# One decoder layer on one core: the halo copy ahead of the scaling, and every up-projection block of the first pass unsplit

## The chip, the core and the metric

The kernel is one program on one core of a Trainium2 chip. It has five instruction streams that run beside each other: TensorE (PE in the profile, with its weight loads on a row of their own, PEld), VectorE (DVE), ScalarE (ACT), GpSimd (POOL) and SyncE (SP), which here issues every DMA. Each stream works in its own order; semaphores tie them together. The metric is the device time of one execution in microseconds, and lower is better.

## What is computed

One layer of a hybrid decoder runs over 2048 prompt tokens and 64 sample tokens (8 sequences of 8) that share all weights. Width is 1024, the feed-forward width 2816. Cut to what matters here:

```
h = rmsnorm(x);  u = h @ w_in                          # mixer: convolutions, delta rule
x = x + concat(conformer, deltanet) @ w_out
up, ffn_buf_new = causal_dwconv(rmsnorm(x) @ w_up, ffn_buf, ffn_conv_w, ffn_conv_b)   # 3 taps
gate, val = split(up, 2)
x = x + (silu(gate) * val) @ w_down
x = x + (p @ w_ple) * sigmoid(x @ w_ple_gate)
return rmsnorm(x) and the new states
```

`w_up` is 1024 x 5632. The three-tap convolution over time needs, for each of the 5632 channels, the last two up-projected columns of the tokens before.

## The kernel before

**Passes.** The tokens go through in six passes of 2, 3, 3, 3, 3 and 2 tiles of 128 (`NTS`, L30); the last one also takes the 64 sample tokens. Channels lie on partitions and tokens run along the free axis, so a pass is `n` = 256, 384, 384, 384, 384 and 320 columns wide. While a pass does its feed-forward, the mixer of the pass after it is merged between the steps (L1437).

**Split weights.** A full-precision product is made of three products in the reduced type `F32R`: a weight block of 128 x 1024 comes as float32 (`raw`, 512 KB), ACT rounds it to a high half, POOL subtracts to get the low half (`split`, L230), and `gemm` (L282) multiplies high by high, high by low and low by high: 24 matmuls for a block of eight 128-deep pieces. The two halves, 1 MB together, are written to DRAM (`halves`, L255), and later passes read them back instead of splitting again. All of this is in `wblock` (L242).

**Unsplit blocks.** In the first pass three of four `w_up` blocks go another way (L243): the float32 block is loaded straight into the weight tile `w`, and `up_gemm` (L1218) multiplies it in plain float32 by `q.hf`, the float32 copy of the normed input that only this pass keeps. There are 44 `w_up` blocks, 22 for gates and 22 for values; 33 of them go unsplit. The set `seen` remembers them: at its next use, in the second pass, such a block is loaded as `raw`, split, and its halves are written. The other 11, those with the block number a multiple of four, are split in the first pass and read back as halves in the second.

**Buffers.** The tile `w` has three buffers, and so has `xio`, which `raw` shares with input rows, output rows and the layer-norm tiles. `get` (L262) keeps three blocks loaded ahead. SP issues every load and store in one order and waits in it: a store of halves waits for POOL's part of the split, and what stands behind it waits too.

**A feed-forward step.** `half` (L1224) takes one `w_up` block: the gemm into a PSUM bank `g` (three buffers, columns 2 onward), the copy of the two halo columns from `ffh` into columns 0 and 1 (L1230, ACT), the scaling by tap 2 with the bias into `y` (L1231, ACT), the two other taps as multiply-adds on DVE that read the bank (L1239), and the copy of the bank's last two columns into `ffh` for the next pass (L1242, ACT). `gate` then applies Silu to `y`, `val` multiplies by the gate on DVE and splits the product into `fbuf` (ACT the high half, POOL the low), and `down` (L1258) multiplies by `w_down` and adds into `X`. The down steps of a group of two are queued one group later.

The framework schedules the recorded instructions engine by engine, so the order on an engine is not that of the source.

Of the kernel before, what the change touches and what calls it, by code (L numbers as in the profile page):

```python
# [16 lines left out]
P = 128  # L17
# [25 lines left out]
def step_kernel(  # L43
# [63 lines left out]
    def act(out, in_, f=AF.Copy, **kw):  # L107
        A.activation(out, in_, f, **kw)  # L108
# [99 lines left out]
    ffh = const([P, 2 * FT, 2 + 2 * NSQ], name="ffh")  # L208
# [28 lines left out]
    halves, seen = {}, set()  # L237
# [2 lines left out]
        return wp.tile([P, 2, KD, P], F32R, tag="w", name=nm("w"), bufs=3)  # L240

    def wblock(key, src, hi_e="a", lo_e="g", nk=KD):  # L242
        if key[0] == "w_up" and key[1] // P % 4 and key not in seen:  # L243
            seen.add(key)
            w = wp.tile([P, KD, P], F32, tag="w", name=nm("w"), bufs=3)
            SY.dma_start(w, src)
            return w
        w = w_tile()
        if key in halves:
            SY.dma_start(w.bitcast(F32), halves[key])  # L250
        else:
            raw = raw_tile("raw")
            SY.dma_start(raw if nk == KD else raw.rearrange("p (k o) c -> p k (o c)", k=nk), src)
            split(raw, w[:, 0], w[:, 1], hi_e, lo_e)
            halves[key] = hw.tile([P, 2, KD, P], F32, tag=nm("halves"), name=nm("halves"))  # L255
            SY.dma_start(halves[key], w.bitcast(F32))
        return w[:, 0], w[:, 1]
# [949 lines left out]
    def units_f(q):  # L1207
        n, np_, sam = q.n, q.np, q.sam
        out = []
        z = {}  # L1210

        def begin():
            z["f"] = big.tile([P, 2 * FG * 2 * NMAX], F32R, tag="F", name=nm("fbuf"))
            if sam:
                z["st"] = big.tile([P, 2 * FT, 2 * NSQ], F32, tag="zs", name=nm("fst"))
                load_T("fst", [st_ffn[0].rearrange("s r c -> (s r) c")], 2 * DFF, z["st"])

        def up_gemm(ps, w):  # L1218
            if isinstance(w, tuple):
                return gemm_w(ps, w, halfs(q.hT2), 0, n)  # L1220
            for k in range(KD):
                mm(ps, w[:, k, :], q.hf[:, k, :], k == 0, k == KD - 1, skip=False)

        def half(col):  # L1224
            ffS = W["ff"]
            w = get()
            y = r_tile("y")
            ps = gbank()
            up_gemm(ps[:, 2:2 + n], w)
            act(ps[:, 0:2], ffh[:, col, 0:2])  # L1230
            act(y[:, :n], ps[:, 2:2 + n], AF.Identity, scale=ffS[:, col, 2:3], bias=ffS[:, col, 3:4])  # L1231
            if sam:
                srow = srow_tile()
                G.tensor_copy(srow[:, :, 0:2], z["st"][:, col, :].rearrange("p (s r) -> p s r", r=2))
                act(srow[:, :, 2:2 + LSQ], sv(ps[:, 2 + np_:2 + n]))
                G.tensor_copy(ffh[:, col, 2:18].rearrange("p (s r) -> p s r", r=2), srow[:, :, 8:10])
            for tap in (1, 0):
                c = ffS[:, col, tap:tap + 1]
                stt(V, y[:, 0:np_], ps[:, tap:tap + np_], c, y[:, 0:np_], MUL, ADD)  # L1239
                if sam:  # L1240
                    stt(V, sv(y[:, np_:n]), srow[:, :, tap:tap + LSQ], c, sv(y[:, np_:n]), MUL, ADD)
            act(ffh[:, col, 0:2], ps[:, np_:np_ + 2])  # L1242
            return y

        def ff_ap(slot, hl, j, a, b):
            base = ((slot * FG + j) * 2 + hl) * NMAX
            return z["f"][:, base + a:base + b]

        def gate(f):
            z["g"] = y = half(f)  # L1250
            act(y[:, :n], y[:, :n], AF.Silu)

        def val(f, slot, j):
            y = half(FT + f)
            tt(V, y[:, :n], y[:, :n], z["g"][:, :n], MUL)
            split(y[:, :n], ff_ap(slot, 0, j, 0, n), ff_ap(slot, 1, j, 0, n))

        def down(nk, slot, i):  # L1258
            w = get()
            m = KD // nk  # L1260
            for o in range(m):
                ps = bank() if q.ip == 0 and o % 2 else gbank()
                gemm(ps[:, :n], (lambda k: w[0][:, k * m + o, :], lambda k: w[1][:, k * m + o, :]),
                     (lambda k: ff_ap(slot, 0, k, 0, n), lambda k: ff_ap(slot, 1, k, 0, n)), nk)
                xs = q.X[:, i * m + o, 0:n]
                tt(V, xs, xs, ps[:, :n], ADD)

        out.append(((), begin))
        pend = []
        for g0 in range(0, FT, FG):  # L1270
            slot = (g0 // FG) % 2
            nk = min(FG, FT - g0)
            for j in range(nk):
                f = g0 + j
                out.append(((("w_up", f * P),), lambda f=f: gate(f)))
                out.append(((("w_up", (FT + f) * P),), lambda f=f, slot=slot, j=j: val(f, slot, j)))
            out += pend
            pend = [((("down", g0, i),), lambda nk=nk, slot=slot, i=i: down(nk, slot, i)) for i in range(nk)]
        return out + pend
# [191 lines left out]
```

## Time and profile before

| what | value |
|---|---|
| median of three runs | 3144.91 us (3142.12 to 3147.45) |
| profiled execution | 3150.69 us, span 3149.0 us |
| busy PE / PEld / DVE / ACT / POOL | 94% / 92% / 67% / 34% / 21% of the span |
| mean granted TensorE clock | 0.974 |
| moved by DMA | 745.19 MB, mean 237 GB/s |
| chain that ended last | PE 65%, DVE 7%, DMA 4%, ACT 1% |

Busy time of PE is of modelled matmul ends, so the start of one row to the start of the next is the better measure of what a block takes. In the time line, the number in brackets at a row's end is how long the engine sat idle before it and for what. The profiled execution took 5.8 us longer than the median of the runs.

In the span, the first pass does its feed-forward from about 332 to 627 us, the second from about 723 to 1192 us; the third, fourth and fifth follow at 522 us each, and the last feed-forward ends at about 3090 us.

### The profile page before, as it was taken

Reading aid. Unit: us, or ns where it says so; the run is one execution under the profiler, and the core shown is the slowest. Engines: PE = TensorE matmul, PEld = TensorE weight load, DVE = VectorE, ACT = ScalarE, POOL = GpSimd, SP = SyncE. Lnnn points to the kernel's source line nnn. Section 1 sums busy time; section 2 is a strip of 40 time slices with the busy share of each in tenths; the row PEclk is TensorE's granted clock in tenths of the full one; section 3 lists DMA queues with packets and bytes.
Section 4 is the critical chain, followed back from the end, with each engine's and each line's share of the span. In section 5 each row is a group of like instructions: output and inputs, shape, how many; then the busy total and the mean of one; then the engine's idle time right before and its main releaser. Section 6 shows DMA issues by size and latency. Waiting matters only on the chain.

```text
span 3149.0 us, 49670 instructions
## 1 busy us (share of the span) xinstructions
PE 2968.5 (94%) x18418; PEld 2888.1 (92%) x18418; DVE 2121.8 (67%) x5378; ACT 1074.2 (34%) x2702; POOL 664.2 (21%) x957
## 2 busy tenths in 40 slices
PE   5979899787999999999999999999999999998998
PEld 5979788787998999999999999999999999898998
DVE  6986889755776686668567656857577866743444
ACT  3434333434222443422234332223342222423223
POOL 3422343334222422200101210110131110111111
PEclk8989899988999999999999999999999999998999
DMA  7645888577786767666756577765677775666885
GB/s 227 202 135 198 247 249 271 204 261 268 263 270 233 272 227 250 247 240 237 236 205 230 205 274 244 242 216 197 238 250 249 258 250 189 221 231 227 297 294 211
DMA packets 300407, 745.19 MB, mean 237 GB/s; under 512 B 51241, under 2 KB 213546, under 8 KB 225023
## 3 DMA queue, kind: packets, MB, share of 16 engines
q1 hardware_dynamic: 300167, 742.03, 68.7%
q8 instruction: 146, 2.39, 0.3%
q14 instruction: 94, 0.77, 0.1%
HBM read 607.75 MB, written 134.57 MB: 236 GB/s over the span
## 4 chain that ended last, share of the span: by engine, by line
PE 65%; DVE 7%; DMA 4%; ACT 1%; issue 1%; POOL 0%; SPq 0%; ACTq 0%; DVEq 0%
PE g L89 57%; PE d L89 3%; DMA w<-halves 3%; PE m L89 2%; PE d L93 1%; DVE h L96 1%; PE m L93 1%; DVE y L96 1%; DMA raw<-in_w_up_dram 1%; DVE cacc L96 0%; DVE H L96 0%; DVE X L100 0%; DVE hT L105 0%; DVE tv L105 0%; DVE X L105 0%
## 5 line engine op out<-in xcount | busy, mean ns | idle before, releaser
L89 PE MATMUL g<-hT,w 128*128 128x384 f32 (+2 forms) x9048 | 1575.3, 332 | 35.6 <-ACT hT L108 9.4
L89 PEld LDWEIGHTS g<-hT,w 128*128 128x128 f32 x9048 | 1499.2, 190 | 46.7 <-ACT hT L108 11.1
L89 PE MATMUL g<-fbuf,w 128*128 128x384 f32 (+2 forms) x2904 | 535.1, 334 | 20.7 <-ACT w L108 8.3
L96 DVE SCALAR_TENSOR_TENSOR y<-g,ffS,y 128x384 f32<-128x384 f32 (+1 forms) x528 | 300.7, 570 | 332.3 <-ACT y L108 244.5
L89 PEld LDWEIGHTS g<-fbuf,w 128*128 128x128 f32 x2904 | 478.6, 189 | 30.2 <-ACT ffh L108 8.9
L96 DVE SCALAR_TENSOR_TENSOR cacc<-H,cfS,cacc 128x384 f32<-128x384 f32 (+1 forms) x696 | 453.0, 651 | 10.3 <-ACT cacc L108 3.1
L105 DVE TENSOR_TENSOR X<-X,g 128x384 f32<-128x384 f32 (+2 forms) x532 | 276.3, 524 | 244.7 <-PE g L89 241.9
L105 POOL TENSOR_TENSOR fbuf<-y,fbuf 128x384 fp32r<-128x384 f32 (+2 forms) x132 | 136.1, 1031 | 716.4 <-ACT fbuf L108 676.4
L105 POOL TENSOR_TENSOR w<-raw,w 128x1024 fp32r<-128x1024 f32 x90 | 218.6, 2430 | 297.7 <-ACT w L108 284.6
L89 PE MATMUL g<-mx,w 128*128 128x384 f32 (+2 forms) x1152 | 198.6, 332 | 15.9 <-DMA w<-halves 15.6
L89 PEld LDWEIGHTS g<-mx,w 128*128 128x128 f32 x1152 | 191.8, 195 | 17.8 <-issue 11.5
L89 PE MATMUL g<-x,w 128*128 128x384 f32 (+2 forms) x1152 | 202.5, 329 | 5.9 <-ACT w L108 4.6
L108 ACT ACTIVATE g<-ffh 128x2 f32<-128x2 f32 x264 | 45.7, 173 | 444.0 <-PE g L89 441.8
L89 PEld LDWEIGHTS g<-x,w 128*128 128x128 f32 x1152 | 190.4, 194 | 6.7 <-ACT w L108 5.0
L108 ACT ACTIVATE y<-g,ffS 128x384 f32<-128x384 f32 (+2 forms) x264 | 169.7, 643 | 13.5 <-ACT g L108 0.4
L108 ACT ACTIVATE ffh<-g 128x2 f32<-128x2 f32 x264 | 45.2, 171 | 351.2 <-DVE y L96 351.2
L89 PE MATMUL g<-hf,w 128*128 128x256 f32 x528 | 125.4, 392 | 7.1 <-DMA w<-in_w_up_dram 3.7
L108 ACT ACTIVATE w<-raw 128x1024 fp32r<-128x1024 f32 x106 | 111.6, 1052 | 57.3 <-PE g L89 18.7
L89 PEld LDWEIGHTS g<-hf,w 128*128 128x128 f32 x528 | 101.1, 197 | 21.4 <-DVE X L105 3.3
L96 DVE SCALAR_TENSOR_TENSOR H<-row,dnS,H 128x384 f32<-128x384 f32 (+1 forms) x144 | 93.4, 650 | 36.9 <-ACT H L108 35.8
L105 POOL TENSOR_TENSOR y<-row,y 128x256 fp32r<-128x256 f32 x48 | 36.9, 768 | 304.2 <-PE m L89 231.9
L503 POOL COPY dnh<-row 128x3 f32<-128x3 f32 x72 | 23.0, 320 | 361.2 <-ACT row L108 361.0
(344 smaller groups left out, 3366.5 us busy)
## 6 DMA issues: line engine op xcount, KB each, us to landing
w<-halves SPq DMA_DIRECT2D x477, 1024.0 KB
halves<-w SPq DMA_DIRECT2D x106, 1024.0 KB
raw<-in_w_up_dram SPq DMA_DIRECT2D x44, 512.0 KB
w<-in_w_up_dram SPq DMA_DIRECT2D x33, 512.0 KB
raw<-in_w_in_dram SPq DMA_DIRECT2D x24, 512.0 KB
raw<-in_w_down_dram SPq DMA_DIRECT2D x22, 512.0 KB
xt<-in_x_prompt_dram SPq DMA_DIRECT2D x16, 512.0 KB
xT<-xt SPq DMA_DIRECT2D x16, 512.0 KB
```

The costliest lines, as they stand in the source:

```text
L89: T.matmul(out, lhsT=lhsT, rhs=rhs, start=start, stop=stop, skip_group_check=skip)
L93: T.transpose(out, in_, ident[:k, :k])
L96: return e.scalar_tensor_tensor(out=out, in0=in0, scalar=scalar, in1=in1, op0=op0, op1=op1)
L105: e.tensor_tensor(out=out, in0=a, in1=b, op=op)
L108: A.activation(out, in_, f, **kw)
L503: G.tensor_copy(dnh[:, j, 0:3], row[:, np_:np_ + 3])
```

## The change

Two edits.

```
--- before.py
+++ after.py
@@ -240,7 +240,7 @@
     def wblock(key, src, hi_e="a", lo_e="g", nk=KD):
-        if key[0] == "w_up" and key[1] // P % 4 and key not in seen:
+        if key[0] == "w_up" and key not in seen:
             seen.add(key)
             w = wp.tile([P, KD, P], F32, tag="w", name=nm("w"), bufs=3)
             SY.dma_start(w, src)
@@ -1228,6 +1228,7 @@
             ps = gbank()
             up_gemm(ps[:, 2:2 + n], w)
             act(ps[:, 0:2], ffh[:, col, 0:2])
+            act(ffh[:, col, 0:2], ps[:, np_:np_ + 2])
             act(y[:, :n], ps[:, 2:2 + n], AF.Identity, scale=ffS[:, col, 2:3], bias=ffS[:, col, 3:4])
...
@@ -1239,7 +1240,6 @@
                 stt(V, y[:, 0:np_], ps[:, tap:tap + np_], c, y[:, 0:np_], MUL, ADD)
...
-            act(ffh[:, col, 0:2], ps[:, np_:np_ + 2])
             return y
```

The first edit sends all 44 `w_up` blocks of the first pass through plain float32; all 44 are then loaded, split and written in the second pass. The second puts the copy into `ffh` ahead of the scaling, in all six passes.

On ACT, in the feed-forward of the third pass, a value block and a gate block stand like this before (`g` is the PSUM bank, `y` the scaled block, `sq` and `H` belong to the mixer of the next pass, the last row is Silu):

```order
L108 ACTIVATE g_18510<-ffh 128x2 [waits PE_49]
L108 ACTIVATE y_18509<-g_18510,ffS 128x384 [waits Activation_49]
L108 ACTIVATE sq_18558<-H_2971_18187 128x384 [waits DVE_49]
L108 ACTIVATE ffh<-g_18510 128x2 [waits DVE_49]
L108 ACTIVATE fbuf_18152<-y_18509 128x384 [waits DVE_49]
L108 ACTIVATE g_18596<-ffh 128x2 [waits PE_49]
L108 ACTIVATE y_18595<-g_18596,ffS 128x384 [waits Activation_49,Pool_49]
L108 ACTIVATE ffh<-g_18596 128x2 [waits DVE_49]
L108 ACTIVATE y_18595<-y_18595 128x384
```

The copy into `ffh` waits for DVE, whose taps read the same bank; Silu behind it has no wait of its own. The same blocks in the changed kernel:

```order
L108 ACTIVATE g_18334<-ffh 128x2 [waits PE_49]
L108 ACTIVATE ffh<-g_18334 128x2 [waits Activation_49]
L108 ACTIVATE y_18333<-g_18334,ffS 128x384
L108 ACTIVATE sq_18382<-H_2971_18011 128x384 [waits DVE_49]
L108 ACTIVATE fbuf_17976<-y_18333 128x384 [waits DVE_49]
L108 ACTIVATE g_18420<-ffh 128x2 [waits PE_49]
L108 ACTIVATE ffh<-g_18420 128x2 [waits Activation_49]
L108 ACTIVATE y_18419<-g_18420,ffS 128x384 [waits Pool_49]
L108 ACTIVATE y_18419<-y_18419 128x384 [waits DVE_49]
```

The copy no longer waits for DVE; Silu (the last row) and the copy into `fbuf` now do.

On SP, at the end of the first pass's feed-forward before (`w<-in_w_up` is an unsplit block, `raw` a block that will be split, `X<-xT` the next pass's input):

```order
L253 DMA raw_6085<-in_w_up_dram 128x8x128
L246 DMA w_6141<-in_w_up_dram 128x8x128
L256 DMA halves_6089<-w_6084 128x2048
L246 DMA w_6207<-in_w_up_dram 128x8x128
L246 DMA w_6274<-in_w_up_dram 128x8x128
L1169 DMA X_6572<-xT_309 128x3072
L253 DMA raw_6303<-in_w_down_dram 128x2x512
L253 DMA raw_6365<-in_w_down_dram 128x2x512
L1308 DMA row_7127<-in_w_ple_dram 128x2x128
L253 DMA raw_6394<-in_w_down_dram 128x2x512
L256 DMA halves_6307<-w_6302 128x2048
L253 DMA raw_6449<-in_w_down_dram 128x2x512
```

and in the changed kernel:

```order
L246 DMA w_5874<-in_w_up_dram 128x8x128
L246 DMA w_5926<-in_w_up_dram 128x8x128
L246 DMA w_5992<-in_w_up_dram 128x8x128
L246 DMA w_6043<-in_w_up_dram 128x8x128
L253 DMA raw_6072<-in_w_down_dram 128x2x512
L253 DMA raw_6134<-in_w_down_dram 128x2x512
L1169 DMA X_6341<-xT_309 128x3072
L256 DMA halves_6076<-w_6071 128x2048
L253 DMA raw_6163<-in_w_down_dram 128x2x512
L1308 DMA row_6896<-in_w_ple_dram 128x2x128
L253 DMA raw_6218<-in_w_down_dram 128x2x512
```

Two of the last four `w_down` loads now stand ahead of `X<-xT`; before, all four stood behind it.

On SP, where the second pass's feed-forward sets in, before (`w_7380<-halves` is the first up block, read back as halves; `w_7863<-halves` is another):

```order
L250 DMA w_7380<-halves_3596 128x2048
L256 DMA halves_7221<-w_7216 128x2048
L370 DMA xt_7344<-in_x_prompt_dram 128x1024
L256 DMA halves_7302<-w_7297 128x2048
L1374 DMA w_7455<-halves_ba 128x1024
L399 DMA xT_7086<-xt_7344 1024x1x128
L253 DMA raw_7565<-in_w_up_dram 128x8x128
```

and in the changed kernel:

```order
L370 DMA xt_7113<-in_x_prompt_dram 128x1024
L256 DMA halves_7071<-w_7066 128x2048
L253 DMA raw_7150<-in_w_up_dram 128x8x128
L399 DMA xT_6855<-xt_7113 1024x1x128
L1374 DMA w_7229<-halves_ba 128x1024
L256 DMA halves_7154<-w_7149 128x2048
L253 DMA raw_7339<-in_w_up_dram 128x8x128
```

The first up block of that pass is now a `raw` load with a split and a store behind it, where a read of halves stood.

## Rows read from the trace of the kernel before

**Rows 1.** Stretches: PE, PEld, DVE, ACT, POOL busy us, clock, DMA share, GB/s.
```profile
332.00:632.00 300.00, 260.19 (x1632) 236.63 (x1632) 252.88 (x557) 121.33 (x327) 115.02 (x103) 0.95 0.76 239
723.00:1205.90 482.90, 459.62 (x2714) 450.31 (x2713) 338.19 (x748) 174.41 (x410) 139.64 (x141) 0.98 0.75 255
1290.00:1726.00 436.00, 432.46 (x2617) 427.55 (x2614) 290.98 (x703) 140.58 (x361) 51.37 (x100) 1.00 0.67 235
2900.00:3046.00 146.00, 146.00 (x1000) 145.09 (x999) 66.48 (x182) 44.60 (x142) 25.14 (x70) 1.00 0.83 297
```

**Rows 2.** Waits of PE, 326 to 640 us: us in total, times, longest us.
```profile
PE g L89 <- ACT w L108: 8.6, 2, 8.3
PE g L89 <- ACT ffh L108: 7.1, 5, 3.8
PE m L89 <- DVE X L105: 6.0, 3, 2.7
PE g L89 <- DMA w<-halves: 5.2, 1, 5.2
...
PE g L89 <- DMA w<-in_w_up_dram: 3.7, 4, 1.2
...
PE m L89 <- ACT w L108: 1.4, 1, 1.4
```

**Rows 3.** Time line of PE, first pass's feed-forward: start us, us, what.
```profile
345.45 7.17 PE L89 MATMUL g<-hf,w 128*128 128x256 f32 x32 [0.25 <-ACT ffh L108]
352.53 3.07 PE L89 MATMUL g<-hT,w 128*128 128x256 f32 x24
355.44 3.62 PE L89 MATMUL g<-hf,w 128*128 128x256 f32 x16
...
460.52 3.18 PE L89 MATMUL g<-hT,w 128*128 128x256 f32 x24
463.54 3.62 PE L89 MATMUL g<-hf,w 128*128 128x256 f32 x16
466.99 0.38 PE L93 MATMUL d<-ident,T 128*128 128x128 f32 x2
```

**Rows 4.** Waits over the span, and two rows of ACT's time line.
```profile
ACT ffh L108 <- DVE y L96: 351.2, 222, 5.2
PE g L89 <- ACT ffh L108: 13.5, 8, 3.8
1380.82 0.17 ACT L108 ACTIVATE ffh<-g 128x2 f32<-128x2 f32 x1 [2.03 <-DVE y L96]
1380.88 0.52 ACT L108 ACTIVATE y<-y 128x384 f32<-128x384 f32 x1
```

**Rows 5.** End of the first pass's feed-forward: time lines of SP and PE.
```profile
601.31 0.34 SPq L1169 DMA_DIRECT2D X<-xT  x1
601.70 0.94 SPq L253 DMA_DIRECT2D raw<-in_w_down_dram  x2
610.48 1.22 PE L89 MATMUL g<-fbuf,w 128*128 128x256 f32 x4 [8.33 <-ACT w L108]
632.61 6.62 PE L89 MATMUL g<-mx,w 128*128 128x384 f32 x24 [5.23 <-DMA w<-halves]
```

**Rows 6.** Waits of PE, 723 to 1192 us.
```profile
PE g L89 <- DMA w<-halves: 4.4, 6, 2.1
...
PE g L89 <- POOL w L105: 2.3, 2, 1.4
...
PE g L89 <- ACT w L108: 1.2, 1, 1.2
```

**Rows 7.** Shorter stretches, columns as in rows 1.
```profile
603.00:632.60 29.60, 14.18 (x100) 13.45 (x100) 19.27 (x47) 17.09 (x33) 18.30 (x13) 0.85 0.87 328
750.00:775.00 25.00, 23.32 (x128) 22.16 (x128) 8.50 (x12) 10.46 (x22) 13.97 (x12) 1.00 1.02 345
```

**Rows 8.** SP's own waits, 723 to 1190 us.
```profile
SPq L256 <- POOL w L105: 170.9, 27, 12.8
```

More of the change, by code (lines that the diff above doesn't have):

```diff
@@ L242, in wblock @@
     def wblock(key, src, hi_e="a", lo_e="g", nk=KD):
-        if key[0] == "w_up" and key[1] // P % 4 and key not in seen:
+        if key[0] == "w_up" and key not in seen:
             seen.add(key)
@@ L1230, in half @@
             act(ps[:, 0:2], ffh[:, col, 0:2])
+            act(ffh[:, col, 0:2], ps[:, np_:np_ + 2])
             act(y[:, :n], ps[:, 2:2 + n], AF.Identity, scale=ffS[:, col, 2:3], bias=ffS[:, col, 3:4])
@@ L1241, in half @@
                     stt(V, sv(y[:, np_:n]), srow[:, :, tap:tap + LSQ], c, sv(y[:, np_:n]), MUL, ADD)
-            act(ffh[:, col, 0:2], ps[:, np_:np_ + 2])
             return y
```

## The prediction

> **What bounds the kernel now.** I read the stretches of the passes first [rows 1]. In the third pass's feed-forward TensorE is busy 432.46 of 436.00 us at a granted clock of 1.00, and in the last pass's 146.00 of 146.00. There TensorE is the bound, and nothing that happens on ACT or in the DMA queues is worth anything unless it makes TensorE wait. The first pass is different: 260.19 of 300.00 us, with DVE busy 252.88, so TensorE and DVE share the bound and 40 us of TensorE's time are idle. The second pass lies between: 459.62 of 482.90, idle 23.3 us against 3.5 in the third pass, with POOL busy 139.64 instead of 51.37, because it splits 33 weight blocks. The first edit acts in these two passes alone, the second in all.
>
> Then I read what TensorE waited for. In the first pass [rows 2] it is late weights (3.7 us for unsplit blocks, 8.6 and 1.4 us for ACT's part of a split, nearly all of the 8.6 at one place) and late releases of banks (7.1 us put down to the halo copy, 6.0 to the adds into X). In the second pass [rows 6] the waits for weights are 4.4, 2.3 and 1.2 us, 7.9 in all.
>
> **Edit one, first pass.** Eleven blocks change from 24 reduced matmuls to float32 ones. From start to start [rows 3], two float32 blocks take 352.53 - 345.45 = 7.08 us, 3.54 each, and the split block behind them 2.91; further on the split block takes 3.02 and the float32 block 3.45. The difference is 0.63 and 0.43, mean 0.53, so 11 x 0.53 = 5.8 us more work on TensorE (4.7 to 6.9). TensorE is busy 87% of this stretch, and what falls into its waits for DVE costs nothing, so I count **+5.0**, with 0 to 6.9 as ends.
>
> The Trainium skill, page "FP8 and Floating Point Precision", section "TensorE Precision Notes", says that true float32 takes four passes through the array. Against the three products of the split that would be a third more, 3.95 us for a float32 block and about +10.9 for eleven, and the sum below would end 5.9 higher. The rows give 3.45 to 3.54 and not 3.95, so I keep them.
>
> What the first pass sheds is eleven splits on ACT and POOL and eleven stores of 1 MB, each of which SP waits for in line. With them go most of the waits for late weights: 3.7 + 1.4 + 0.3 (the rest of the 8.6) = 5.4 us [rows 2]. I take **-4.0** (0 to -5.4), since two splits of `w_down` a group stay.
>
> At the end of that feed-forward stands the one long wait: SP issued X<-xT at 601.31, when the last float32 matmul had released the buffer, and only behind it the last loads of `w_down`; TensorE stood for 8.33 us, until 610.48 [rows 5]. The new order on SP has two of the four loads ahead of X<-xT. Their blocks give TensorE 48 matmuls, 2 x 2.91 = 5.8 us of work. The third block now stands where the first stood, right behind X, and that one came 8.33 us after TensorE ran dry: 8.33 - 5.8 = 2.5 us of wait are left. In between, though, SP now has a store of 1.05 MB, 3.2 us at the 328 GB/s of this stretch [rows 7], which may push it to 5.7. The gain is 2.6 to 5.8, and I take **-4.3** (ends 0 to -8.3). What is late next is the first w_out block: TensorE waited 5.23 us for it at 632.61, and since its load waits for a weight buffer that the down steps free, it moves along with them.
>
> The clock is the last term here: the granted clock in 603 to 632.6 us was 0.85 [rows 7], between its two levels of 1.2 and 2.4 GHz after the long wait, and the 24 matmuls at 632.61 took 6.62 us. A shorter wait gives some of that back: **-1.5** (0 to -3).
>
> **Edit one, second pass.** Eleven blocks change from a read of halves (1.05 MB) to a raw load (0.52 MB), a split and a store (1.05 MB). The bound from below: the waits for weights of 7.9 us over 33 split blocks are 0.24 each, so 2.6 us. From above within the same mechanism: all of the extra idle time, 23.3 - 3.5 = 19.8 us, over 33 is 0.6 each, so 6.6 us. I take **+4.5**. The cover is that three blocks are kept loaded ahead and that POOL has 340 us free in this pass. What it costs if that is gone is the first rival. The queue that feels it is SP's: it already stands 170.9 us in this pass behind 27 waits of a store for POOL [rows 8], and every read of halves behind such a store waits too.
>
> **Edit two.** ACT waited 351.2 us for DVE's taps ahead of the halo copy [rows 4], the largest wait of ACT that a step of this edit touches. It is not gone but handed on: Silu stands right behind the copy and needs the same taps (the copy waited 2.03 us to 1380.82, Silu ran at 1380.88), and on a value block the copy into fbuf needs the taps and the product. The new order shows just that: the wait for DVE is now on Silu and fbuf. What is gained is that the bank is released by the second tap and not by a copy of 0.17 us behind it. TensorE waited for that release 8 times, 13.5 us in all [rows 4], but most of each is DVE being late, not the copy; 8 x 0.25 = 2 us is the gain. Against it the scaling, and so the first tap, starts up to 0.17 us later in each block, which matters where DVE is the bound, in the first pass. Net **-1.0** (-13.5 to +2). In the third to the last pass it is nothing, since TensorE does not wait there.
>
> **Sum.** 5.0 - 4.0 - 4.3 - 1.5 + 4.5 - 1.0 = -1.3 us. The profiled execution took 3150.69 us, so it would take 3149.4; it stands 5.8 above the median of the runs, and against the median of 3144.91 that is **3143.5**. A measurement of this kernel can tell about 0.2%, 6.3 us, from no change: from 3138.6 to 3151.2 is the same.
>
> **Rivals.** *The second pass becomes bound by its weights (slower).* In 750 to 775 us the DMA share was 1.02 at 345 GB/s [rows 7]: there the engines were full. If every one of the eleven blocks meets full engines, its 0.52 MB more cost 0.52 / 0.345 = 1.52 us, 16.7 in all instead of 4.5, and the time is 3144.91 - 5.8 + 16.7 = 3155.8. It decides from about eight blocks exposed (12.1 us). For it speaks that SP's order doesn't let later reads pass a waiting store; against it that the share over the whole stretch is 0.75 [rows 1], and that 11 x 0.52 = 5.8 MB come to 255 GB/s x 482.9 us = 123 MB. The Trainium skill, page "DMA: Bandwidth & Descriptors", section "Bandwidth", puts the limit of HBM for one core near 358 GB/s; the 345 GB/s of the row agree, and by its figure the eleven would cost 16.1.
>
> *The first pass swallows the work (faster).* If TensorE's extra work falls mostly into its waits for DVE (+1 instead of +5.0), all late weights go (-5.4) and the second pass's cover holds (+1 instead of +4.5), the sum is 1 - 5.4 - 4.3 - 1.5 + 1 - 1 = -10.2, 3134.7. DVE's 252.88 of 300.00 us speak for it; against it that the adds into X, the wait for DVE that has a name in rows 2, come to 6.0 us in one row, hardly more than what would have to be swallowed.
>
> *The halo copy's wait was the cause and not the sign (faster).* If the 13.5 us on the copy vanish whole, the sum is -13.8, 3131.1. The 351.2 us look like it; the order with its waits speaks against it. The opposite, that the edit removes no wait from the path at all, is what the forecast takes nearly as given.
>
> **How the numbers follow.** The forecast, within 0.2%: 0.49. Weights bound the second pass: 0.24. The first pass swallows the work: 0.21. The halo copy: 0.06. So faster 0.27, same 0.49, slower 0.24. The forecast's own range is 3138 to 3151; the range that should hold 8 in 10 takes in both main rivals with a little of the spread of a median, 3132 to 3158, and leaves out the far ends of the halo and of the DMA.
>
> **What the profile after would show.** Right: the first pass's feed-forward up to some 6 us shorter, with the wait at its end cut to about 4 us; the second pass's longer by 2 to 7 us, 44 splits in it and more waits of TensorE for halves; ACT's wait for DVE now ahead of Silu and fbuf with a total near 300 us; the third to sixth passes unchanged within 1 us each. Wrong: TensorE's float32 blocks taking other than 3.4 to 3.6 us; the long wait at the end of the first pass still whole, or turned into a wait for X; a DMA share near 1 over long parts of the second pass; or a change in the later passes.

## The result: 3125.4 us, faster than the whole forecast range

The changed kernel takes 3125.39 us (median, 3122.79 to 3127.08) beside 3143.51 for the kernel before on the same chip, a ratio of 0.9941 with a 95% interval of 0.9923 to 0.9958: 18 us less. The forecast was 3143.5 with a range from 3132 to 3158, and "within 0.2%" as the likeliest outcome. The profiled execution of after has a span of 3125.4 us beside 3149.0, so 23.6 us are to be found between the two traces.

To find them I cut both spans at the same places, the last matmul of the `w_out` blocks of each pass (`g<-mx,w` on TensorE's time line), and behind the first pass's feed-forward also at the first `w_out` matmul, which is the second pass's. A period is named by the pass whose feed-forward it holds and ends with the `w_out` of the pass after. All numbers of the table are from the profiled executions, one for each kernel, in us; the last three columns are the timed runs. Each ratio is to runs of before that were taken with that kernel's (medians from 3143.5 to 3147.1 us), so it is not the quotient of two medians in this table.

| kernel | first feed-forward | w_out behind it | 2nd period | 3rd period | 4th period | 5th period | to the end | median us | ratio to before | interval |
|---|---|---|---|---|---|---|---|---|---|---|
| before | 308.5 | 36.1 | 558.2 | 522.3 | 522.0 | 521.4 | 356.3 | 3143.51 | 1 | |
| after | 287.0 | 40.2 | 561.2 | 517.1 | 516.7 | 520.7 | 358.4 | 3125.39 | 0.9941 | 0.9923 to 0.9958 |
| e1_halo | 301.8 | 38.2 | 552.9 | 516.9 | 516.4 | 518.8 | 358.9 | 3131.03 | 0.9964 | 0.9951 to 0.9978 |
| e2_unsplit | 287.1 | 35.9 | 562.2 | 522.8 | 521.7 | 521.7 | 357.8 | 3132.53 | 0.9961 | 0.9947 to 0.9975 |
| e3_xt_act | 308.9 | 36.6 | 553.9 | 522.6 | 521.1 | 519.1 | 356.1 | 3144.04 | 0.9996 | 0.9986 to 1.0007 |
| e4_unsplit22 | 317.3 | 35.3 | 544.4 | 521.7 | 519.0 | 518.4 | 358.3 | 3139.99 | 0.9992 | 0.9981 to 1.0003 |
| e10_halo_34 | 308.5 | 36.2 | 561.1 | 517.1 | 519.4 | 519.4 | 356.0 | 3135.68 | 0.9970 | 0.9961 to 0.9980 |
| e8_pool_free | 296.3 | 35.4 | 554.1 | 521.8 | 522.7 | 521.5 | 358.3 | 3134.35 | 0.9962 | 0.9948 to 0.9975 |
| e9_pool_load | 296.5 | 39.6 | 558.2 | 517.3 | 518.1 | 518.9 | 358.3 | 3133.92 | 0.9962 | 0.9947 to 0.9976 |
| e11_no_store | 298.6 | 36.7 | 563.5 | 523.0 | 522.5 | 521.6 | 358.8 | 3142.34 | 0.9989 | 0.9977 to 1.0000 |
| e5_hf_own | 290.3 | 36.9 | 562.4 | 517.0 | 517.6 | 520.5 | 359.5 | 3127.96 | 0.9944 | 0.9931 to 0.9957 |
| e12_down_dve | 279.0 | 35.6 | 556.4 | 518.0 | 516.3 | 520.0 | 356.2 | 3113.61 | 0.9898 | 0.9881 to 0.9915 |
| e13_down_up_dve | 281.1 | 36.5 | 553.9 | 517.4 | 517.2 | 522.0 | 359.1 | 3110.74 | 0.9890 | 0.9875 to 0.9905 |

From before to after: -21.5 in the first feed-forward, +4.1 in the `w_out` behind it, +3.0 in the second period, -5.2 in the third, -5.3 in the fourth, -0.7, +2.1. Two things happened that the forecast didn't have: the first feed-forward gained more than four times the first pass's sum of -4.8, and two later periods, on which I had put nothing, gained 5 us each. How far one profile can be trusted shows in the second period: the kernels with 33 blocks unsplit and the same splits there read 552.9 to 561.1, so single differences of some us in that column mean little.

### The profile page after: what moved, and what is told of

Same layout as the page of the kernel before. It is cut to its first block, busy times and chain, and to the rows that moved or that the text cites. A ratio compares the mean times of both kernels' runs of the same rounds, so it can differ in the third digit from the quotient of the medians.

```text
span 3125.4 us, 49428 instructions
## 1 busy us (share of the span) xinstructions
PE 2963.4 (95%) x18330; PEld 2880.4 (92%) x18330; DVE 2121.9 (68%) x5378; ACT 1064.5 (34%) x2704; POOL 660.8 (21%) x957
## 4 chain that ended last, share of the span: by engine, by line
PE 75%; DVE 14%; DMA 6%; ACT 2%; issue 1%; POOL 1%; SPq 0%; POOLq 0%; DVEq 0%; ACTq 0%
PE g L89 65%; PE d L89 4%; PE m L89 3%; DMA w<-halves 3%; DVE cacc L96 2%; DVE y L96 2%; PE d L93 1%; PE m L93 1%; DVE h L96 1%; DVE tv L105 1%; DVE H L96 1%; DVE rt L105 1%; DMA w<-in_w_up_dram 1%; DVE X L105 1%; POOL w L105 1%
## 5 line engine op out<-in xcount | busy, mean ns | idle before, releaser
L89 PE MATMUL g<-hT,w 128*128 128x384 f32 (+2 forms) x8784 | 1534.2, 332 | 29.7 <-ACT t L108 8.1
L89 PEld LDWEIGHTS g<-hT,w 128*128 128x128 f32 x8784 | 1461.8, 190 | 38.4 <-ACT t L108 8.5
L89 PE MATMUL g<-hf,w 128*128 128x256 f32 x704 | 161.2, 383 | 3.4 <-DMA w<-in_w_up_dram 2.9
L89 PEld LDWEIGHTS g<-hf,w 128*128 128x128 f32 x704 | 131.7, 192 | 21.0 <-DMA w<-in_w_up_dram 1.5
L108 ACT ACTIVATE fbuf<-y 128x384 fp32r<-128x384 f32 (+2 forms) x132 | 65.9, 499 | 201.9 <-DVE y L105 201.2
L108 ACT ACTIVATE y<-y 128x384 f32<-128x384 f32 (+2 forms) x132 | 65.7, 498 | 199.2 <-DVE y L96 198.8
L96 DVE SCALAR_TENSOR_TENSOR H<-row,dnS,H 128x384 f32<-128x384 f32 (+1 forms) x144 | 94.4, 656 | 38.2 <-ACT H L108 36.3
```

What stands on the lines that cost most here:

```text
L89: T.matmul(out, lhsT=lhsT, rhs=rhs, start=start, stop=stop, skip_group_check=skip)
L96: return e.scalar_tensor_tensor(out=out, in0=in0, scalar=scalar, in1=in1, op0=op0, op1=op1)
```

## The profile after

First the first feed-forward, in stretches of before and after (columns: stretch, us, busy us and instructions of PE, PEld, DVE, ACT, POOL, granted clock, DMA share, GB/s). Before:

```profile
324.10:632.60 308.50, 262.02 (x1640) 238.08 (x1640) 258.03 (x575) 121.75 (x328) 119.93 (x108) 0.94 0.76 240
```

After, with the second period behind it:

```profile
324.10:611.10 287.00, 260.98 (x1553) 235.57 (x1553) 240.48 (x570) 109.63 (x314) 90.12 (x95) 0.97 0.69 214
...
651.30:1212.50 561.20, 521.70 (x3105) 509.56 (x3104) 402.89 (x863) 213.11 (x482) 193.57 (x175) 0.96 0.79 267
```

TensorE's busy time in the feed-forward is 1 us less, although eleven blocks went to float32; the gain is idle time, 46.5 us before and 26.0 after. POOL lost 29.8 us, most of it eleven subtractions. But DVE lost 17.6 us too, and neither edit takes an operation from DVE: 575 and 570 instructions. Its groups say which became cheaper (DVE's groups over the same stretches, busy us, mean ns, idle before). Before:

```profile
L96 DVE SCALAR_TENSOR_TENSOR cacc<-H,cfS,cacc 128x384 f32<-128x384 f32 x116 | 88.6, 764 | 1.6
L96 DVE SCALAR_TENSOR_TENSOR y<-g,ffS,y 128x256 f32<-128x256 f32 x88 | 42.0, 479 | 23.5 <-ACT y L108 22.9
...
L105 DVE TENSOR_TENSOR y<-y,y 128x256 f32<-128x256 f32 x22 | 18.3, 831 | 1.3 <-ACT y L108 1.1
```

After:

```profile
L96 DVE SCALAR_TENSOR_TENSOR cacc<-H,cfS,cacc 128x384 f32<-128x384 f32 x116 | 83.5, 720 | 2.0 <-ACT cacc L108 0.4
L96 DVE SCALAR_TENSOR_TENSOR y<-g,ffS,y 128x256 f32<-128x256 f32 x88 | 42.2, 479 | 26.8 <-ACT y L108 26.0
...
L105 DVE TENSOR_TENSOR y<-y,y 128x256 f32<-128x256 f32 x22 | 13.9, 632 | 0.2
```

The taps `y<-g,ffS,y`, which read a PSUM bank, take 479 ns in both. The product `y<-y,y` and the mixer's convolution `cacc`, whose two tensor inputs both lie in SBUF, take less in after, where POOL has less to do.

Such a mean mixes two kinds. One place in the trace of before, from the time lines of POOL, DVE and PE:

```profile
401.19 2.38 POOL L105 TENSOR_TENSOR w<-raw,w 128x1024 fp32r<-128x1024 f32 x1 [4.43 <-ACT w L108]
401.40 2.59 DVE L96 SCALAR_TENSOR_TENSOR cacc<-H,cfS,cacc 128x384 f32<-128x384 f32 x1
404.91 0.60 DVE L96 SCALAR_TENSOR_TENSOR cacc<-H,cfS,cacc 128x384 f32<-128x384 f32 x1
405.90 2.08 PE L89 MATMUL m<-H 128*128 128x128 f32 x8 [2.72 <-DVE X L105]
407.77 5.77 PE L89 MATMUL g<-hf,w 128*128 128x256 f32 x16
```

The first `cacc` starts 0.21 us after a subtraction of weights on POOL, takes 2.59 us and ends 0.42 us after the subtraction. The second meets none and takes 0.60. The adds into X stand behind the first one; TensorE waits 2.72 us for them, and the 16 float32 matmuls next take 5.77 us at a granted clock of 0.62, where such a block takes 3.62 in [rows 3]. Over the first feed-forward of before, the 89 `cacc` that overlap no elementwise operation of POOL take 613 ns on average and 656 at most, and the 27 that overlap one take 1259 and 2670; for the taps it is 477 and 482 ns on average. So a mean over all says how often they met, and need not follow POOL's busy time: `y<-y,y` takes 581 ns in e4_unsplit22, where POOL is busy 146 us, and 831 before with 120.

What TensorE still waits for there (us in all, times, longest), as [rows 2] before:

```profile
PE d L93 <- DVE on L100: 4.6, 3, 2.4
PE g L89 <- DVE y L96: 4.1, 3, 1.8
PE g L89 <- ACT w L108: 4.0, 2, 2.2
PE m L89 <- DVE dg L100: 3.4, 1, 3.4
PE g L89 <- DMA w<-in_w_up_dram: 2.9, 4, 1.4
```

The wait on the halo copy is now called a wait on DVE's tap, 7.1 us before and 4.1 after. The waits for unsplit blocks hardly moved (3.7 to 2.9).

The float32 blocks (TensorE's groups, same stretches). Before:

```profile
L89 PE MATMUL g<-hf,w 128*128 128x256 f32 x528 | 125.4, 392 | 7.1 <-DMA w<-in_w_up_dram 3.7 <-DVE X L105 3.1 <-ACT ffh L108 0.2
...
L89 PE MATMUL g<-hT,w 128*128 128x256 f32 x264 | 36.2, 289 | 1.6 <-ACT hT L108 1.0 <-ACT w L108 0.3 <-POOL hT L105 0.3
```

After:

```profile
L89 PE MATMUL g<-hf,w 128*128 128x256 f32 x704 | 161.2, 383 | 3.4 <-DMA w<-in_w_up_dram 2.9 <-DVE hf L96 0.6
```

44 blocks took 125.4 + 36.2 = 161.6 us before and 161.2 after. A float32 block is dearer than a split one (3.80 us against 3.29 in before). But the granted clock over these matmuls alone was 0.97 before and 0.99 after; e2_unsplit had 0.98 there and 162.1 us, though its clock over the whole stretch was 0.94 as before. At the full clock this would be about 157 us before and 160 in the other two, by my estimate from these figures: some 3 us more work, and the clock paid for it.

The end of that feed-forward, as [rows 5]. SP's time line of after:

```profile
571.65 1.11 SPq L253 DMA_DIRECT2D raw<-in_w_down_dram  x2
582.85 0.34 SPq L1169 DMA_DIRECT2D X<-xT  x1
587.46 0.34 SPq L256 DMA_DIRECT2D halves<-w  x1
588.14 0.38 SPq L253 DMA_DIRECT2D raw<-in_w_down_dram  x1
```

And TensorE's:

```profile
584.99 0.73 PE L89 MATMUL g<-fbuf,w 128*128 128x256 f32 x4 [2.17 <-ACT w L108]
587.66 0.45 PE L93 MATMUL d<-ident,on 128*128 128x128 f32 x1 [1.94 <-DVE on L100]
590.55 0.47 PE L93 MATMUL d<-ident,on 128*128 128x128 f32 x1 [2.44 <-DVE on L100]
```

Two `w_down` loads do stand ahead of X<-xT, and the one wait of 8.33 us became several short ones. From the last float32 matmul's end to the first `w_out` matmul it was 632.6 - 601.3 = 31.3 us and is 611.1 - 582.8 = 28.3.

ACT's waits over the span, as [rows 4], with the halo copy gone from the list:

```profile
ACT fbuf L108 <- DVE y L105: 201.2, 108, 4.3
ACT y L108 <- DVE y L96: 198.8, 113, 8.8
```

Before, these two rows stood at 63.4 and 9.2 us, so 327 of the copy's 351.2 us were handed on to them.

And SP's wait for POOL in the second feed-forward (711 to 1178 us), as [rows 8]:

```profile
SPq L256 <- POOL w L105: 219.4, 38, 13.0
```

## The experiments

**Each edit alone.** e1_halo moves the halo copy in the kernel before:

```
             act(ps[:, 0:2], ffh[:, col, 0:2])
+            act(ffh[:, col, 0:2], ps[:, np_:np_ + 2])
...
-            act(ffh[:, col, 0:2], ps[:, np_:np_ + 2])
```

> The kernel before with the halo copy moved, weights split as before. Theory: the two edits act in different places. The halo copy alone leaves the first pass where it was (its last w_out block ends at 668.7 us before, I expect 665 to 670), and takes about 5 us out of the third pass (522.3 us from one last w_out block to the next before, 517.1 with both edits), because on SP the next w_out load now stands ahead of the second load of x; in the fourth pass the same, unless the third load of x, which still stands behind three weight loads there, undoes it. Sum -5 to -11 us. Rival, the wait on the halo copy was the cause of everything: the first pass 13 us or more shorter and the whole gain of about 18 to 24 us here already. Second rival, the halo copy does nothing: every pass within 1 us of before.

e2_unsplit changes the condition alone:

```
-        if key[0] == "w_up" and key[1] // P % 4 and key not in seen:
+        if key[0] == "w_up" and key not in seen:
```

> The kernel before with all 44 up blocks of the first pass unsplit, the halo copy at its old place. Theory: the first pass gets nearly all that it got with both edits (last w_out block ending near 651 instead of 668.7 us), the second pass gets 3 us longer (561.2 instead of 558.2), and the third and fourth stay at 522 us since SP's order keeps the second load of x ahead of the w_out load. Sum about -14 us. Rival: without the halo edit TensorE still waits the 7 us on the halo copy in the first pass and gains only half of the 17 us; sum about -5. Second rival, the gain of the third and fourth passes comes with this edit: they are 517 us each.

The third and fourth periods are 516.9 and 516.4 with the halo edit and 522.8 and 521.7 without: they belong to it. The first feed-forward is 287.1 with the unsplit edit alone, as with both, so its 21.5 us belong to that one. The halo edit alone shortens the split form by 6.7 there, which I had not expected; once the blocks are unsplit it adds nothing. The `w_out` stage behind is longer in these two profiles with it, 38.2 and 40.2 us against 35.9 and 36.1, but that doesn't belong to the edit: e5, e12 and e13 carry it too and take 36.9, 35.6 and 36.5. So the two edits overlap in the first feed-forward. The times, 0.36% and 0.39% alone and 0.59% together, can't tell an overlap from a plain sum within their intervals.

**Where the later passes' gain comes from.** At the end of the third period stands the fourth pass's `w_out`. In both traces TensorE takes its first three blocks in pieces, since half of their input (`mx` from `zs`) is late. The fourth block's weights need a buffer that one of these three holds, and there the kernels differ. TensorE's time line before:

```profile
1709.06 4.18 PE L89 MATMUL g<-mx,w 128*128 128x384 f32 x22
...
1716.81 6.50 PE L89 MATMUL g<-mx,w 128*128 128x384 f32 x36
1723.15 0.38 PE L93 MATMUL m<-ident,pt 128*128 128x128 f32 x2
1726.33 5.98 PE L89 MATMUL g<-mx,w 128*128 128x384 f32 x24 [2.80 <-DMA w<-halves]
```

SP's before:

```profile
1709.25 0.32 SPq L250 DMA_DIRECT2D w<-halves  x1
1718.77 0.56 SPq L399 DMA_DIRECT2D xT<-xt  x1
1720.91 1.19 SPq L250 DMA_DIRECT2D w<-halves  x2
```

TensorE's after:

```profile
1693.46 2.25 PE L89 MATMUL g<-mx,w 128*128 128x384 f32 x12
...
1698.86 8.57 PE L89 MATMUL g<-mx,w 128*128 128x384 f32 x48
1707.27 0.38 PE L93 MATMUL m<-ident,pt 128*128 128x128 f32 x2
1708.56 0.93 PE L89 MATMUL g<-mx,w 128*128 128x384 f32 x4 [0.91 <-DVE pT L105]
```

SP's after:

```profile
1693.66 0.32 SPq L250 DMA_DIRECT2D w<-halves  x1
1700.83 0.56 SPq L399 DMA_DIRECT2D xT<-xt  x1
1703.65 1.36 SPq L250 DMA_DIRECT2D w<-halves  x2
```

Counted from the first `w_out` matmul, the fourth block's load is issued at 11.85 us before (1720.91 - 1709.06) and at 10.19 after; TensorE has run out of work at 14.5 and 14.2. From the issue to the fourth block's first matmul it is 5.42 us before (1720.91 to 1726.33) and 4.91 after (1703.65 to 1708.56), so TensorE waits 2.80 us in the one and 0.91 in the other, where the profile names DVE. Before, the granted clock was 0.99 in the wait and 0.70 in the 5.6 us behind it:

```profile
1723.40:1726.30 2.90, 0.13 (x2) 0.01 (x1) 1.54 (x4) 0.91 (x2) 0.00 (x0) 0.99 0.99 387
1726.30:1731.90 5.60, 5.58 (x23) 5.60 (x24) 0.00 (x0) 0.00 (x0) 0.00 (x0) 0.70 0.88 369
```

24 matmuls took 5.98 us there, where 48 take 8.57 after, 4.3 for 24. So the wait cost 2.8 + 1.7 = 4.5 us, against 0.9 after: 3.6 of the 5.2 us.

What holds the load up? Before, SP stood 9.1 us ahead of the store xT<-xt, and the load stands behind it. That was my first theory. e3_xt_act issues this store from ACT:

```
-            SY.dma_start(q.xT[:, :, c0:c0 + L], ...)
+            A.dma_start(q.xT[:, :, c0:c0 + L], ...)
```

> The kernel before with one change that neither edit makes: the store of the transposed x (xT<-xt) is issued by ACT and not by SP. Theory: in the third and fourth passes TensorE's wait for the fourth w_out block (2.80 us at 1726.33, 3.27 us in the next pass) comes from SP standing 9.1 us before that store, for ACT's copy, with the block's load behind it. Taken off SP's queue, both waits and the slow matmuls behind them go: each of the two passes 4 to 6 us shorter, the fifth perhaps as well (a wait of 4.31 us there). Sum -8 to -15 us. Rival: it is the load of x ahead of the weight loads, or the DMA engines, that makes the block late: then the passes stay at 522 us within 1 us.

It fell: 522.6 and 521.1, ratio 0.9996. With the store gone SP waits for TensorE itself, until 1719.05 by its trace, 13.4 us after the first `w_out` matmul at 1705.64, and two waits of TensorE for halves (1.52 and 2.54 us) are still there. The buffer is what is late, not the queue. The second of these waits stands where the 2.80 us stood:

```profile
1724.20 8.01 PE L89 MATMUL g<-mx,w 128*128 128x384 f32 x44 [2.54 <-DMA w<-halves]
```

The granted clock behind it was 1.00, and 44 matmuls took 8.01 us, 4.4 for 24. So the slow clock need not follow such a wait, and the period is as long as before without it.

What the halo edit changed is the order that the scheduler gives TensorE: before, twelve matmuls of each of the first three blocks come ahead of the thirteenth of the first; now the first block goes on after twelve of the second and is given back earlier. And on SP the first of these weight loads now stands ahead of the second load of x. To see whether this hangs on the edit in these passes alone, e10_halo_34 moves the copy only there:

```
+            early = q.ip in (2, 3)
+            if early:
+                act(ffh[:, col, 0:2], ps[:, np_:np_ + 2])
...
+            if not early:
                 act(ffh[:, col, 0:2], ps[:, np_:np_ + 2])
```

> The kernel before with the halo copy moved in the third and fourth passes alone. Theory: what the halo edit gives in these passes is the order of the next w_out blocks (the third block is begun later, the first given back earlier, so that the fourth block's weights are asked for about 1.7 us earlier, and the w_out load stands ahead of the second load of x on SP). Then the two periods are 517 us each (522.3 and 522.0 before), and the first and second passes stay as they were, 668.7 within 2 us and 553 to 559 us. Sum -10. Rival: what e1 showed there is chance of the profile: 520 to 522.

517.1 and 519.4 (in the fourth, half of the gain that I expected), the first feed-forward 308.5 as before, and 0.30% in all, nearly what e1 gives altogether. The load comes 10.2 us after the first `w_out` matmul, as in after. So these two periods' gain comes with the halo edit's own order in them, a gain of the schedule and not of ACT's work. Which of the two moves counts, TensorE's pieces or SP's load of x, I did not separate.

**What the unsplit blocks took away.** e4_unsplit22 goes the other way, 22 unsplit:

```
-        if key[0] == "w_up" and key[1] // P % 4 and key not in seen:
+        if key[0] == "w_up" and key[1] // P % 2 and key not in seen:
```

> The kernel before with 22 of the 44 up blocks unsplit in the first pass instead of 33. Theory: the first pass's time goes with the number of splits and stores in it, so that the last w_out block ends 10 to 20 us later than 668.7, and the second pass, with eleven blocks fewer to split, is 2 to 4 us shorter than 558.2; sum +8 to +16. Rival: the first pass gained only from what stood in SP's order at its end, and eleven splits more cost it nothing: it ends within 4 us of 668.7, and the sum is about -3.

The first feed-forward is 317.3 us: 8.8 for the step from 22 to 33 unsplit and 21.5 for the step from 33 to 44, in a row but not in proportion; the second period is 13.8 shorter, far more than I expected and not explained here, and the total is the same instead of 8 to 16 us longer. DVE's `cacc` takes 836, 764 and 720 ns with 22, 33 and 44, and POOL is busy 146, 120 and 90 us. That led to DVE. e8_pool_free keeps the eleven splits and their stores but lets ACT write both halves, and leaves out the subtraction:

```
-            split(raw, w[:, 0], w[:, 1], hi_e, lo_e)
+            if key[0] == "w_up" and key[1] // P % 4 == 0:
+                act(w[:, 0], raw)
+                act(w[:, 1], raw)
+            else:
+                split(raw, w[:, 0], w[:, 1], hi_e, lo_e)
```

> The kernel before, with 11 up blocks of the first pass split as before, but the low half written by ACT as a second copy (so the low halves of these blocks hold wrong values) and not by POOL's subtraction. TensorE's matmuls, the stores and SP's loads are those of before. Theory: POOL's work on SBUF slows DVE's instructions that read and write SBUF alone (cacc took 836, 764 and 712 to 720 ns on average with 22, 11 and no split up blocks in the first pass's feed-forward), DVE bounds much of that stretch, and this is what the unsplit blocks took away. Then cacc falls to 715 to 730 ns here, DVE's busy time from 256.7 to 240 to 245 us, and the stretch from the first w_out's end to the next w_out's start (308.5 us before, 287.0 with both edits) to 290 to 298. Rival, the loads and stores of the splits, in SP's line, made TensorE wait: the stretch stays within 4 us of 308.5 though DVE gets faster. The kernel as a whole -10 to -18 by the theory, 0 to -4 by the rival.

`cacc` falls to 715 ns, DVE's busy time to 238.3 us, TensorE's idle time from 46.5 to 33.6, and the feed-forward to 296.3: 12.2 of the 21.5.

```profile
322.70:619.00 296.30, 262.69 (x1642) 240.65 (x1641) 238.31 (x575) 133.84 (x339) 94.14 (x97) 0.94 0.80 251
```

This run also spares SP some waits for POOL (117.6 us before, 80.8 for POOL and 13.5 for ACT here, up to 600 us), so I also put the load back. e9_pool_load gives the kernel after ten subtractions on POOL that nobody waits for:

```
             SY.dma_start(w, src)
+            if key[1] // P % 4 == 0 and hasattr(ps_[0], "hT2"):
+                tt(G, ps_[0].hT2[:, 0, :, 0:P], w, w, SUB)
             return w
```

> The kernel after, with ten subtractions of 128x1024 given back to POOL in the first pass's feed-forward: at every fourth up block POOL subtracts the weights from themselves into the buffer of hT2, which no matmul reads in that pass. SP's order is that of after. Theory (POOL's work slows DVE, and DVE holds TensorE): DVE's busy time in the stretch rises from 239.6 to 248 to 256 us and the stretch from 287.0 to 293 to 303. Rival: SP's line and the late weights were what counted: the stretch stays at 287 within 3 us.

Its first feed-forward, and DVE's groups there:

```profile
324.30:620.80 296.50, 269.41 (x1554) 243.01 (x1553) 252.83 (x570) 109.95 (x315) 110.46 (x105) 0.94 0.67 207
...
L96 DVE SCALAR_TENSOR_TENSOR cacc<-H,cfS,cacc 128x384 f32<-128x384 f32 x116 | 91.9, 792 | 2.0 <-ACT cacc L108 0.5
L96 DVE SCALAR_TENSOR_TENSOR y<-g,ffS,y 128x256 f32<-128x256 f32 x88 | 42.1, 478 | 22.0 <-ACT y L108 21.4
```

19.8 us of POOL's work raised DVE's busy time from 240.5 to 252.8, the taps on PSUM stayed at 478 ns, and the feed-forward grew from 287.0 to 296.5. SP's wait for POOL did not change (84.0 and 86.0 us). So ten subtractions on POOL that nobody waits for cost this stretch 9.5 us. How they reach TensorE shows only in part: its idle time grew from 26.0 to 27.1 us, and the rest is busy time, 261.0 to 269.4, at a granted clock of 0.94 instead of 0.97. Nor is the cost even. The 13th up block starts 72.0 us into the stretch in after and 79.9 in e9, so 8 of the 9.5 us are there by then; before it started at 87.1, and 15 of the 21.5 us are.

The other half goes with the stores. e11_no_store splits and multiplies the eleven blocks as before, but stores no halves (the second pass splits them again):

```
+            if key[0] == "w_up" and key not in seen:
+                seen.add(key)
+                return w[:, 0], w[:, 1]
             halves[key] = hw.tile(...)
             SY.dma_start(halves[key], w.bitcast(F32))
```

> The kernel before with the 11 split up blocks of the first pass split as before and multiplied as halves, but their halves not stored; the second pass loads and splits them itself, as in after. This takes away the 11 stores and SP's waits for POOL ahead of them, and leaves POOL's subtractions. If what is left of the first pass's gain beside POOL's work on DVE (21.5 us in all, of which the runs with POOL freed and POOL loaded show 10 to 12) sits in SP's line, the stretch from the first w_out's end to the next w_out's start falls from 308.5 to 297 to 302 us; if it sits in ACT's share of the splits, in the matmuls themselves or in the clock, it stays at 305 to 309. In the second pass 44 splits: 559 to 563 us. In all -8 to +4.

```profile
323.30:622.00 298.70, 259.89 (x1642) 237.12 (x1641) 256.60 (x575) 121.12 (x328) 119.34 (x108) 0.95 0.68 211
```

298.6, 9.9 less than before, with DVE nearly as busy as before (256.6 us). Together with e9's value for eleven, 10.5, this makes 20.4 of the 21.5 us, if the two simply add up, which no run tests. Whether the stores cost by SP's standing in line or by their 11 MB on the DMA engines (the share fell from 0.76 to 0.68) is open.

**Versions that go further.** e5_hf_own drops the split of the normalised input that no matmul of the first pass reads any more, and keeps `hf` in its buffer, so that X<-xT waits for no up block:

```
-            q.hT2 = big.tile([P, 2, KD, NMAX], F32R, tag="hT2", name=nm("hT2"))
+            q.hT2 = big.tile([P, 2, KD, NMAX], F32R if q.ip else F32, tag="hT2", name=nm("hT2"))
...
-                    q.hf = big.tile([P, KD, n], F32, tag="X", name=nm("hf"), bufs=2)
-                h = q.hf[:, b]
+                h = q.hT2[:, 0, b]
```

> The kernel after, with the split of the normalised input dropped in the first pass, where no matmul reads it any more, and the fp32 input hf kept in that buffer, so that the load of the next X waits for no last up block. Theory: eight copies on ACT and eight subtractions on POOL and DVE fewer at the start of the stretch, and no wait for X at its end: the stretch 287.0 us becomes 278 to 284, the rest as in after; sum -3 to -9 against after, so 3116 to 3122 beside 3125. Rival: the end is bound by the last splits of w_down, which nothing here touches, and the time stays within 3 us of after.

No gain: 290.3 us instead of 278 to 284, and with the `w_out` behind it 290.3 + 36.9 = 327.2 us, the 327.2 of after. TensorE's first wait behind the last up block is still 2.17 us, for ACT's part of a split. The wait for X's load was not on the path. e12_down_dve takes the lesson of e8 and e9 and puts the low halves of `w_down` on DVE:

```
-            return wblock(key, rows[...], nk=nk)
+            return wblock(key, rows[...], lo_e="v", nk=nk)
```

> The kernel after, with the subtraction for the low halves of the 22 w_down blocks (all in the first pass's feed-forward) on DVE (1.22 us each where DVE does it for w_in and w_out) and not on POOL (2.38 us each there). Theory: POOL's work costs DVE more than it would cost DVE to do it: ten subtractions on POOL cost DVE 10 us and more, 22 some 25 to 37, against 22 x 1.22 = 26.8 us of its own; and the weights are there 1.2 us earlier. So the stretch of 287.0 us stays or gets up to 8 shorter, 279 to 288. Rival: DVE is the bound and simply gets 27 us more to do: 295 to 310.

DVE's groups in its first feed-forward:

```profile
L96 DVE SCALAR_TENSOR_TENSOR cacc<-H,cfS,cacc 128x384 f32<-128x384 f32 x116 | 72.1, 622 | 1.6 <-ACT cacc L108 0.2
...
L105 DVE TENSOR_TENSOR w<-raw,w 128x1024 fp32r<-128x1024 f32 x22 | 26.9, 1221 | 9.6 <-ACT w L108 9.5
...
L105 DVE TENSOR_TENSOR y<-y,y 128x256 f32<-128x256 f32 x22 | 9.3, 422 | 0.3
```

DVE does 26.9 us of subtractions more and is busy 236.5 us instead of 240.5: its other work got 31 us cheaper. The feed-forward falls to 279.0, and the kernel to 3113.61, 0.9898 of before. The weights are also ready 1.2 us earlier here, and e12 doesn't part that from DVE's gain. e13_down_up_dve does the same to every other up block of the second pass; the `w_gate` blocks that its expectation names stay with POOL:

```
-... lo_e="v" if name in ("w_in", "w_out") and at[0] // P % 2 else "g")
+... lo_e="v" if name in ("w_in", "w_out", "w_up") and at[0] // P % 2 else "g")
```

> As e12, and in the second pass every other one of the 44 up blocks and of the 8 w_gate blocks has its low half made by DVE. There DVE is busy 402.89 of 561.20 us, so it has room. Theory: SP's stores wait for POOL's subtraction (170.9 us over that feed-forward before), and a weight load stands behind each; with the halves there 1.2 us earlier and POOL working on one block in two, the second pass falls from 561.2 to 548 to 557 us. Rival: DVE is late instead for the taps and the adds into X, TensorE waits for these, and the pass stays at 560 or gets longer.

553.9 for the second period against 556.4 in e12, within what profiles differ there, and 0.9890 beside 0.9898, with intervals that overlap. Both beat the change; between the two these runs don't decide.

## Why the prediction was wrong

**The first pass's work, late weights and clock (+5.0, -4.0, part of -1.5).** This is the step that failed. Up to the last float32 matmul the two terms allowed +1.0; the rows give 258.7 against 277.2 us (582.8 and 601.3, from 324.1), -18.5. I read that DVE was busy 252.88 of 300 us [rows 1] and took this for DVE's fixed load, which only made TensorE's extra work cheaper (the second rival, -10.2). But the load itself depends on POOL: eleven subtractions fewer took 17.6 us off DVE. The Trainium skill says why, page "SBUF — State Buffer", section "SBUF: two separate sides": DVE and GpSimd share one pair of ports, held for a whole instruction, and a DVE operation with two SBUF inputs meets a GpSimd one that reads SBUF. The rows agree: two SBUF inputs slowed (720 to 792 ns in e9), a PSUM input not (479 and 478), and a `cacc` that met a subtraction ended 0.42 us after it. They show the size here, 12.3 us of DVE for 19.8 us of POOL. The ceiling of the second term was wrong as well. I capped it by the waits that bear the name of weights, 5.4 us, while e11 shows 9.9 us from the stores alone. There TensorE's waits with the name of weights hardly moved (14.0 and 13.0 us for `ACT w`, `POOL w` and the unsplit loads) and those for the adds into X fell from 10.2 to 4.1; how a store comes to delay an add is not shown. The extra work was there, some 3 us of the 5.8, but was paid by the clock: 161.6 and 161.2 us for all 44 blocks.

**The end of the first feed-forward (-4.3).** Right: 3.0 us, two loads ahead of X<-xT, the long wait split up. The clock's term (-1.5) came and went: the first 24 `w_out` matmuls take 4.43 us in after, at a clock of 1.00, instead of 6.62; but TensorE then waits 1.98 us for halves, and the clock in the 7.1 us behind that wait is 0.59. The stage as a whole got 4.1 longer, which I did not see. e5 has the same wait, 1.97 us, and a stage of 36.9, so most of the 4.1 is that slow clock.

**The second pass (+4.5).** Right in size: +3.0 in these two profiles, and 560.6 against 556.0 as means over all profiles with 44 and with 33 splits there on POOL (after, e2, e5, e9, e11, e12; before, e1, e3, e8, e10), +4.6. The rival that the weights bound it did not come. That waits for weights make the difference is not shown: they come to 13.7 us in before and 16.0 in after, but also to 17.5 and 20.9 in e1 and e10, with the splits of before.

**The halo edit (-1.0, "in the third to the last pass it is nothing, since TensorE does not wait there").** Wrong. This is the second step that failed, a term put at nothing. Of the 3.5 us of idle time that I read in 1290 to 1726 us [rows 1], 2.5 were the wait for the fourth `w_out` block, which the stretch cuts off at its end; that wait and the slow matmuls behind it cost 4.5 us. I compared the orders of the first two passes and took the rest as given, though a scheduler that lays out the whole program may move rows anywhere. In the first feed-forward the edit alone gave 6.7 us (e1) and with the other nothing. That ACT's wait is handed on was right, to Silu and `fbuf`: their rows total 400 us instead of the 300 that I named, since 73 stood there already.

**The forecast's signs.** "Up to some 6 us" for the first pass and "unchanged within 1 us" for the third to sixth are the two that failed; the float32 blocks (3.45 us from start to start, 376.69 to 380.14 in after), the cut of the long wait and the second pass held. The sum itself was 0.1 off: -1.3 from 3144.91 is 3143.6, which changes nothing.

## What to carry to other kernels

When work leaves one engine, ask not only who waited for it but whose instructions it slowed: compare the mean time of the same instruction in stretches where the other engine is busy and where it isn't. An operation on an idle GpSimd is not free if VectorE is a bound, and moving it to VectorE itself can make VectorE less busy. And where a scheduler writes the order, compare the whole of it, above all the few places in the steady passes where TensorE still waits: there a small edit can be worth a wait, and at times a slow clock behind it, in every such pass.

## What the runs showed of the hardware

A DVE instruction with two tensor inputs in SBUF that met an elementwise operation of POOL took about twice as long on average: `cacc` 613 ns without one and 1259 with one, up to 2670, in the first feed-forward of before. Its mean over that stretch was 836 ns in e4 with POOL busy 146 of 317 us and 622 in e12 with 44 of 279. The taps, with a PSUM input, took 477 and 482 ns.

A subtraction of 128x1024 takes 2.4 us on POOL and 1.22 on DVE. For each one on POOL DVE's busy time grew by 0.8 to 1.8 us: 8.7 for eleven from before to e4, 12.3 for ten in e9, 17.6 for eleven between after and before, 19.7 for eleven between e8 and before. The Trainium skill, page "Perfetto Trace Analysis", section "Optimizing Scalar/DVE Operations", says that offloading between these two might not help. The runs agree: with 22 subtractions moved from POOL to DVE in e12, the first feed-forward is 8 us shorter.

A wait of TensorE of 2.8 us was followed by 24 matmuls in 5.98 us instead of 4.3, at a granted clock of 0.70; in e3 one of 2.54 us was followed by matmuls at 1.00.
